# Decoder trunk on one core: scales of the first sub-layer by TensorE products, input load and norm first

## Chip, cores, metric

One core of a Trainium2 chip. The metric is the device time of one execution in microseconds (us), as the median of several runs; for a single execution the profile gives the span from its first to its last instruction.

## The reference

Four layers of a decoder trunk over 256 tokens of width 1024, everything in float32. Each layer has three sub-layers (feed-forward, token mixer, feed-forward). Each sub-layer normalises its input, modulates it with a scale and a shift, computes, normalises again and adds with a gate. Scale, shift and gate are products of silu(c) with slices of a large weight `ada_w` (4 x 1024 x 9216).

```python
cond = jax.nn.silu(c)                                   # (1, 1024)
for i in range(4):
    mod = (cond @ ada_w[i] + ada_b[i]).reshape(B, 3, 3, D)
    def sublayer(x, sidx, fn, res_w):
        shift, scl, gate = mod[:, sidx, 0], mod[:, sidx, 1], mod[:, sidx, 2]   # each [:, None, :]
        hh = rms_norm(x, norm_g[i, 2 * sidx]) * (1.0 + scl) + shift
        return x + res_w * gate * rms_norm(fn(hh), norm_g[i, 2 * sidx + 1])
    x = sublayer(x, 0, lambda hh: swiglu(hh, ffn_w1[i, 0], ffn_w2[i, 0]), 0.5)
    ...
```

What matters here is the very first sub-layer (i = 0, sidx = 0): its shift and scale have to be there before its first matrix product, and nothing runs ahead of it that could hide their making.

## The kernel before, in words

The tokens lie in two halves `h` of 128 (tiles `x0`, `x1`). Every weight is loaded as float32 by the SP queue (`raw_load`, L126, into a ring of 7 buffers of 128x1024, 512 KB each), split by ScalarE into a rounded part `hi` (L135) and by VectorE into the rest `lo` (L136), and multiplied three times on TensorE (hi by yh, hi by yl, lo by yh: L369, L370, L371), where `yh` and `yl` are the same split of the modulated input. A tile framework writes each engine's instructions into one fixed order and sets the semaphores; each engine then runs its own order strictly, and `tc.issue_after` only holds an instruction back in that order.

The start of the program is `Ffn.first` (L465 and on). The conditioning vector is loaded, transposed by TensorE (L85) and put through silu into `cT`, 8 columns of 128 (L86). Five small tiles with norm gains and biases (`g_ld`) come over the ScalarE queue (L104) and are turned by `turn_gains` (five transposes `pt_g` L111, five copies L112 into `abT` and `gT`).

The modulation of the first sub-layer comes in four column blocks `cb` of 512 (0 and 1 the shift, 2 and 3 the scale; 0 and 2 belong to the first half of the width, called n = 0, and 1 and 3 to the second, n = 1). For one block `first_sums(cb)` loads four tiles `raw_ada` of 2 x 128 rows, and VectorE forms the running sum of row times silu(c) in `ada_acc`: eight instructions of 128x512 (the first L265, the others L267). `first_columns` then adds over the partitions on TensorE: four float32 products `p_ada` of a 128x128 piece with a column of ones (L242), and VectorE makes the columns `ab` of them (shift L244; scale L247 and L248).

The input is loaded (L473), `norm_in` squares it on ScalarE (L315), VectorE and GpSimd make the factor `rx` (L307, L308), VectorE the normalised `xn` (L338). TensorE turns it (`p_y`, L322), `modulate` applies `ab` (ScalarE for h = 0, L333; VectorE for h = 1, L331) and splits into `yh` (L334) and `yl` (L335).

With half of the width modulated, half of the products can be done: `products(b, 0)` runs 48 matmuls `p_gu` for each of the first three blocks `b` of the hidden layer (144 in all) over n = 0; in the meantime blocks cb = 1 and 3 are made, n = 1 is modulated, and `products(b, 1)` adds the second half and ends in `hu` (silu on ScalarE, L531).

Of the kernel before, what the change touches and what calls it, by code (L numbers as in the profile page):

```python
# [28 lines left out]
D = 1024  # L29
# [11 lines left out]
def trunk_kernel(ctx, tc, x, c, ada_w, ada_b, norm_g, ffn_w1, ffn_w2, nsa_w_in, nsa_cmp_pe, nsa_cmp_w1,  # L41
# [4 lines left out]
    def dap(t, off, ap):  # L46
        return bass.AP(tensor=t.tensor, offset=t.offset + off, ap=ap)
# [13 lines left out]
    def bank(tag, shape, name):  # L61
        n = {"acc": 4, "mm": 2, "tp": 2}[tag]
        return psum.tile(shape, FT, name=name, tag=tag, bufs=n)
# [58 lines left out]
    def raw_load(ap, shape, name):  # L122
        t = stream.tile([128] + shape, FT, name="raw_" + name, tag="raw", bufs=NRAW)
        aps = ap if isinstance(ap, list) else [(slice(0, 128), ap)]
        for sl, a in aps:
            nc.sync.dma_start(out=t[sl], in_=a)  # L126
        return t
# [106 lines left out]
    def first_columns(cbs):  # L234

        if not AB:
            AB[0, 0] = work.tile([128, 2 * KC], FT, name="ab", tag="ab", bufs=3)
        ab = AB[0, 0]
        for cb, a in cbs:
            p = bank("acc" if cb % 2 == 0 else "tp", [128, 4], "p_ada0")  # L240
            for j in range(4):
                nc.tensor.matmul(p[:, j:j + 1], a[:, j * 128:(j + 1) * 128], ones_col, start=True, stop=True)  # L242
            if cb < 2:
                nc.vector.tensor_add(ab[:, 8 + cb * 4:12 + cb * 4], p, abT[:, cb * 4:cb * 4 + 4])  # L244
            else:
                o = ab[:, cb * 4 - 8:cb * 4 - 4]
                nc.vector.scalar_tensor_tensor(o, p, 1.0, abT[:, cb * 4:cb * 4 + 4], op0=OP.add, op1=OP.add)  # L247
                ins = nc.vector.tensor_mul(o, o, gT[:, cb * 4 - 8:cb * 4 - 4])  # L248
        return ins.ins

    summed = []

    def first_sums(cb):

        a = work.tile([128, 512], FT, name="ada_acc", tag="ada_acc", bufs=NACC)
        for k0 in range(0, KC, 2):
            r = raw_load(dap(ada_w, k0 * 128 * 9 * D + cb * 512, [[9 * D, 128], [128 * 9 * D, 2], [1, 512]]),
                         [2, 512], "ada")
            for j in range(2):
                k = k0 + j  # L260
                with ExitStack() as st:
                    for ins in summed[-1:]:
                        st.enter_context(tc.issue_after(ins))
                    if k == 0:
                        ins = nc.vector.tensor_scalar(a, r[:, j], cT[:, k:k + 1], None, op0=OP.mult)  # L265
                    else:
                        ins = nc.vector.scalar_tensor_tensor(a, r[:, j], cT[:, k:k + 1], a, op0=OP.mult, op1=OP.add)  # L267
                summed.append(ins.ins)
        return a

    def gate_finish(i, s, accs):

# [122 lines left out]
    class Ffn:  # L395
# [70 lines left out]
        def first(self):  # L466

            self.new_hb()
            cbs, xn, ps = {}, [], []
            turn_gains()  # L470
            cbs[0] = first_sums(0)
            for h in range(2):
                nc.sync.dma_start(out=xs[h], in_=x[0, h * 128:(h + 1) * 128, :])  # L473
            cbs[2] = first_sums(2)
            for h in range(2):
                r, _ = norm_in(h)
                xn.append(big([128, D], "xn"))
                for m in range(2):
                    scaled(xn[h], h, m, r)

            def products(b, n):
                for cc in range(2):
                    if not n:
                        ps.append(bank("mm" if b == 0 else "acc", [128, 2, T], "p_gu"))
                    self.gu(ps[2 * b + cc], b, cc, range(KC // 2 * n, KC // 2 * (n + 1)))
                    if n:
                        self.hu(ps[2 * b + cc], b, cc)

            for n in range(2):
                done = summed[-1]  # L490
                gate = first_columns([(cb, cbs[cb]) for cb in (n, n + 2)])
                pt = [turn(xn[h], n) for h in range(2)]
                for h in range(2):
                    modulate(AB[0, 0], pt[h], h, n, h == 1)
                gate_on[:] = [gate] if n else [done]
                if n:
                    products(FIRST - 1, 0)
                    for b in range(FIRST):
                        self.up(b)
                        products(b, 1)  # L500
                else:
                    for b in range(FIRST - 1):
                        self.up(b, part=0)
                        products(b, 0)
                        gate_on[:] = []
                        if not b:
                            cbs[1] = first_sums(1)
                    cbs[3] = first_sums(3)
                    gate_on[:] = [gate]
                    self.up(FIRST - 1, part=0)  # L510
            self.begun = FIRST
            return gate
# [648 lines left out]
```

## Time and profile before

| | us |
|---|---|
| median of 3 runs (2192.07 to 2196.46) | 2192.75 |
| the profiled execution | 2192.57 |
| its span, first to last instruction | 2190.8 |
| TensorE busy in the span (97%) | 2120.4 |
| VectorE, ScalarE busy | 1634.4, 1106.2 |

The span is 1.8 us shorter than the execution around it. Times in the profile are counted from the start of the span. PE is TensorE, PEld its weight loads, DVE is VectorE, ACT is ScalarE, POOL is GpSimd, SP is the engine whose queue issues the weight loads. "idle before" is the time in which an engine stood still ahead of a row, with what released it.

### The profile page before, as it was taken

Reading aid. Unit: us, or ns where it says so; the run is one execution under the profiler, and the core shown is the slowest. Engines: PE = TensorE matmul, PEld = TensorE weight load, DVE = VectorE, ACT = ScalarE, POOL = GpSimd, SP = SyncE. Lnnn points to the kernel's source line nnn. Section 1 sums busy time; section 2 is a strip of 40 time slices with the busy share of each in tenths; the row PEclk is TensorE's granted clock in tenths of the full one; section 3 lists DMA queues with packets and bytes.
Section 4 is the critical chain, followed back from the end, with each engine's and each line's share of the span. In section 5 each row is a group of like instructions: output and inputs, shape, how many; then the busy total and the mean of one; then the engine's idle time right before and its main releaser. Section 6 shows DMA issues by size and latency. Waiting matters only on the chain.

```text
span 2190.8 us, 37402 instructions
## 1 busy us (share of the span) xinstructions
PE 2120.4 (97%) x14427; PEld 1865.7 (85%) x14427; DVE 1634.4 (75%) x2748; ACT 1106.2 (50%) x1965; POOL 69.0 (3%) x154
## 2 busy tenths in 40 slices
PE   5999999999999999999999999999999999999998
PEld 5999866799899979899989888799999997667998
DVE  7987876877798777777687858687778858767654
ACT  3444644644554456744454455664454445555443
POOL 1000000000000000100000000000000000000000
PEclk9999998999999999999999999999999999999999
DMA  9998762588699856388779947278869977625761
GB/s 313 338 347 275 230 170 62 183 287 270 209 328 306 281 192 216 124 284 279 239 253 325 314 161 280 74 256 282 283 188 334 320 230 228 163 71 162 244 199 60
DMA packets 338179, 512.55 MB, mean 234 GB/s; under 512 B 20832, under 2 KB 211256, under 8 KB 338000
## 3 DMA queue, kind: packets, MB, share of 16 engines
q1 hardware_dynamic: 329456, 501.15, 69.2%
q10 hardware_dynamic: 8544, 9.01, 1.4%
q8 instruction: 113, 1.85, 0.3%
q14 instruction: 66, 0.54, 0.1%
HBM read 507.91 MB, written 1.05 MB: 232 GB/s over the span
## 4 chain that ended last, share of the span: by engine, by line
PE 73%; DVE 10%; DMA 6%; issue 5%; ACT 3%; POOL 2%; SPq 0%; ACTq 0%; DVEq 0%; POOLq 0%
PE p_gu L369 11%; PE p_gu L370 11%; PE p_gu L371 11%; PE f L388 6%; PE f L389 6%; PE f L392 6%; DMA raw_ada<-in_ada_w_dram 4%; DVE lo_w L136 3%; PE p_o L818 2%; PE p_s L646 2%; PE p_pr L371 1%; PE p_pr L369 1%; PE p_pr L370 1%; PE p_t L668 1%; DVE ada_acc L192 1%
## 5 line engine op out<-in xcount | busy, mean ns | idle before, releaser
L135 ACT CAST hi_w<-raw_w 128x1024 fp32r<-128x1024 f32 x528 | 551.8, 1054 | 329.1 <-PE f L392 116.2
L136 DVE TENSOR_TENSOR lo_w<-raw_w,hi_w 128x1024 fp32r<-128x1024 f32 x528 | 633.0, 1220 | 103.9 <-ACT hi_w L135 98.4
L369 PE MATMUL p_gu<-yh,hi_w 128*128 128x256 f32 x2368 | 665.8, 281 | 4.0 <-DVE yh L334 4.0
L370 PE MATMUL p_gu<-yl,hi_w 128*128 128x256 f32 x2368 | 661.2, 279 | 0.3 <-DVE yl L335 0.3
L371 PE MATMUL p_gu<-yh,lo_w 128*128 128x256 f32 x2368 | 660.9, 279 | 0.0
L369 PEld LDWEIGHTS p_gu<-yh,hi_w 128*128 128x128 f32 x2368 | 445.9, 188 | 17.3 <-DVE lo_w L136 6.0
L192 DVE SCALAR_TENSOR_TENSOR ada_acc<-raw_ada,cT,ada_acc 128x512 f32<-128x512 f32 x500 | 373.8, 748 | 105.4 <-DMA raw_ada<-in_ada_w_dram 97.3
L370 PEld LDWEIGHTS p_gu<-yl,hi_w 128*128 128x128 f32 x2368 | 446.2, 188 | 5.4 <-issue 1.7
L371 PEld LDWEIGHTS p_gu<-yh,lo_w 128*128 128x128 f32 x2368 | 446.1, 188 | 0.0
L388 PE MATMUL f<-hi_w,hb 128*128 128x512 f32 x704 | 275.7, 393 | 2.5 <-ACT hb L533 2.4
L389 PE MATMUL f<-lo_w,hb 128*128 128x512 f32 x704 | 275.8, 392 | 0.0
L392 PE MATMUL f<-hi_w,hb 128*128 128x512 f32 x704 | 228.2, 391 | 0.0
L533 ACT CAST hb<-sg 128x256 fp32r<-128x256 f32 x148 | 60.2, 407 | 207.8 <-DVE sg L532 206.2
L388 PEld LDWEIGHTS f<-hi_w,hb 128*128 128x128 f32 x704 | 132.2, 188 | 30.1 <-ACT hb L533 5.5
L392 PEld LDWEIGHTS f<-hi_w,hb 128*128 128x128 f32 x704 | 131.6, 188 | 29.1 <-DVE hb L534 1.8
L531 ACT ACTIVATE sg<-p_gu 128x256 f32<-128x256 f32 x148 | 56.2, 380 | 197.5 <-PE p_gu L371 183.2
L389 PEld LDWEIGHTS f<-lo_w,hb 128*128 128x128 f32 x704 | 132.2, 188 | 24.4 <-issue 0.2
L532 DVE TENSOR_TENSOR sg<-sg,p_gu 128x256 f32<-128x256 f32 x148 | 61.5, 415 | 79.5 <-ACT sg L531 79.3
L657 ACT ACTIVATE sc<-sc,sm_m 128x128 f32<-128x128 f32 (+1 forms) x160 | 70.6, 443 | 41.4 <-DVE sm_m L652 41.4
L534 DVE TENSOR_TENSOR hb<-sg,hb 128x256 fp32r<-128x256 f32 x148 | 62.4, 422 | 35.2 <-ACT hb L533 35.2
L333 ACT ACTIVATE y<-p_y,ab 128x128 f32<-128x128 f32 x184 | 67.4, 465 | 33.3 <-PE p_y L322 28.6
L370 PE MATMUL p_pr<-yl,hi_qk 128*128 128x256 f32 x256 | 71.8, 281 | 0.0
(266 smaller groups left out, 3226.6 us busy)
## 6 DMA issues: line engine op xcount, KB each, us to landing
raw_w<-in_ffn_w_dram SPq DMA_DIRECT2D x528, 512.0 KB
raw_ada<-in_ada_w_dram SPq DMA_DIRECT2D x288, 512.0 KB
raw_kv<-in_nsa_w_in_dram SPq DMA_DIRECT2D x16, 512.0 KB
raw_q<-in_nsa_w_in_dram SPq DMA_DIRECT2D x16, 512.0 KB
raw_cw<-in_nsa_cmp_w_dram SPq DMA_DIRECT2D x16, 512.0 KB
raw_wo<-in_nsa_w_out_dram SPq DMA_DIRECT2D x32, 256.0 KB
raw_qk<-in_sb_w_in_dram SPq DMA_DIRECT2D x16, 512.0 KB
raw_qk<-in_diff_w_in_dram SPq DMA_DIRECT2D x16, 512.0 KB
```

What stands on the lines that cost most here:

```text
L135: nc.scalar.copy(hi, src)
L136: nc.vector.tensor_sub(lo, src, hi)
L192: nc.vector.scalar_tensor_tensor(a, r[:, j], cT[:, k:k + 1], a, op0=OP.mult, op1=OP.add)
L333: nc.scalar.activation(y[:, j, :], p[:, j, :], AF.Identity, scale=ab[:, k:k + 1], bias=ab[:, 8 + k:9 + k])
L369: nc.tensor.matmul(o, cols(wh), yh[:, k, :], start=first and k == 0, stop=False)
L370: nc.tensor.matmul(o, cols(wh), yl[:, k, :], start=False, stop=False)
L371: nc.tensor.matmul(o, cols(wl), yh[:, k, :], start=False, stop=last and k == KC - 1)
L388: nc.tensor.matmul(acc[n], lh, wh[:, sl], start=first, stop=False)
L389: nc.tensor.matmul(acc[n], lh, wl[:, sl], start=False, stop=False)
L392: nc.tensor.matmul(acc[n], ll, wh[:, sl], start=False, stop=last)
L534: nc.vector.tensor_sub(hl[:, cc, :], sg, hh[:, cc, :])
L657: nc.scalar.activation(sc[e][:, j, :], sc[e][:, j, :], AF.Exp, bias=m[:, x:x + 1], scale=sl[x], accum_out=l[:, x:x + 1])
```

## The change

Input load and norm move ahead of the modulation weights. The blocks 0 and 2 are loaded in turns (`first_pair`): a tile of block 0, a tile of block 2, and so on. Block 0 is summed on VectorE as before. Block 2 is no longer summed there: for each of its 8 row groups TensorE multiplies the four 128x128 pieces of the raw tile with the column of silu(c), 32 float32 products that add up in one bank `p_mod`, from which `first_columns` takes the scale without a product with ones. The turning of the gains is held back until after the third of the four tiles of block 2. Blocks 1 and 3 are made as before.

```diff
+            if cb == 2:
+                p = a
+            else:
+                p = bank("acc" if cb % 2 == 0 else "tp", [128, 4], "p_ada0")
...
+    def first_pair(then):
+
+        a = work.tile([128, 512], FT, name="ada_acc", tag="ada_acc", bufs=NACC)
+        p = bank("acc", [128, 4], "p_mod")
+        for k0 in range(0, KC, 2):
+            if k0 == KC - 2:
+                with tc.issue_after(ins.ins):
+                    then()
+            first_sum(a, first_load(0, k0), k0)
+            r = first_load(2, k0)
             for j in range(2):
                 k = k0 + j
+                for q in range(4):
+                    ins = nc.tensor.matmul(p[:, q:q + 1], r[:, j, q * 128:(q + 1) * 128], cT[:, k:k + 1],
+                                           start=k == 0 and q == 0, stop=k == KC - 1 and q == 3, skip_group_check=True)
+        return a, p
...
             cbs, xn, ps = {}, [], []
-            turn_gains()
-            cbs[0] = first_sums(0)
             for h in range(2):
                 nc.sync.dma_start(out=xs[h], in_=x[0, h * 128:(h + 1) * 128, :])
-            cbs[2] = first_sums(2)
+            cbs[0], cbs[2] = first_pair(turn_gains)
             for h in range(2):
-                r, _ = norm_in(h)
+                with tc.issue_after(silu):
+                    r, _ = norm_in(h)
```

(`first_load` and `first_sum` are the two halves of the loop of `first_sums`, cut out so that both functions call them.) The change also moves later instructions, since the framework orders each engine anew. Line numbers of the changed kernel are larger: the products are L292, `p_ada` is L245, `ab` L247, L250 and L251, `p_y` L347, `p_gu` L394 to L396.

TensorE's order from the first instruction on, before (`pt_c` turns c):

```order
L85 MATMUL pt_c<-ident,c_67 128x8
L111 MATMUL pt_g<-ident,g_ld 128x96 x5
L322 MATMUL p_y<-ident,xn 128x128 x3
L242 MATMUL p_ada_172<-ones_col,ada_acc 128x1 x4
L322 MATMUL p_y<-ident,xn 128x128 x5
L242 MATMUL p_ada_178<-ones_col,ada_acc 128x1 x4
L369 MATMUL p_gu<-yh,hi_w_211 128x256 x2
```

and in the changed kernel:

```order
L85 MATMUL pt_c<-ident,c_67 128x8
L292 MATMUL p_mod<-cT,raw_ada 128x1 x16
L347 MATMUL p_y<-ident,xn 128x128 x4
L292 MATMUL p_mod<-cT,raw_ada 128x1 x8
L111 MATMUL pt_g<-ident,g_ld 128x96 x5
L347 MATMUL p_y<-ident,xn 128x128 x4
L245 MATMUL p_ada_196<-ones_col,ada_acc 128x1 x4
L292 MATMUL p_mod<-cT,raw_ada 128x1 x8
L394 MATMUL p_gu<-yh,hi_w_230 128x256 x2
```

Thirty-two products stand ahead of the first `p_gu` where four stood (the sums of block 2); the turned gains and all turned inputs stand between them.

VectorE's order before, from the first scale columns to the sums of block 1 (`lo` of the first two weight tiles, then the modulation of n = 0):

```order
L136 TENSOR_TENSOR lo_w_212<-raw_w_209,hi_w_211 128x1024
L247 SCALAR_TENSOR_TENSOR ab<-p_ada_178,abT 128x4
L136 TENSOR_TENSOR lo_w_218<-raw_w_215,hi_w_217 128x1024
L248 TENSOR_TENSOR ab<-ab,gT 128x4
L265 TENSOR_SCALAR ada_acc<-raw_ada,cT 128x512
L331 TENSOR_SCALAR y<-p_y,ab 128x128 x4
L334 CAST yh<-y 128x4x128 x2
L335 TENSOR_TENSOR yl<-y,yh 128x4x128 x2
L267 SCALAR_TENSOR_TENSOR ada_acc<-raw_ada,cT,ada_acc 128x512 x3
```

and in the changed kernel:

```order
L250 SCALAR_TENSOR_TENSOR ab<-p_mod,abT 128x4
L251 TENSOR_TENSOR ab<-ab,gT 128x4
L356 TENSOR_SCALAR y<-p_y,ab 128x128 x4
L359 CAST yh<-y 128x4x128 x2
L360 TENSOR_TENSOR yl<-y,yh 128x4x128 x2
L136 TENSOR_TENSOR lo_w_231<-raw_w_228,hi_w_230 128x1024
L136 TENSOR_TENSOR lo_w_237<-raw_w_234,hi_w_236 128x1024
L267 TENSOR_SCALAR ada_acc<-raw_ada,cT 128x512
L269 SCALAR_TENSOR_TENSOR ada_acc<-raw_ada,cT,ada_acc 128x512 x7
```

The two `lo` of the first weights and the first sum of block 1, which stood ahead of the modulation, now stand behind it. Further down, where n = 1 is modulated, one more `lo` has moved ahead of the last `yl`; VectorE's order there in the changed kernel (`cvalid` is a constant of a later layer):

```order
L251 TENSOR_TENSOR ab<-ab,gT 128x4
L1115 TENSOR_SCALAR cvalid_711<-cdist_709 128x15
L1115 TENSOR_SCALAR cvalid_718<-cdist_716 128x15
L136 TENSOR_TENSOR lo_w_389<-raw_w_386,hi_w_388 128x1024
L356 TENSOR_SCALAR y<-p_y,ab 128x128 x2
L136 TENSOR_TENSOR lo_w_395<-raw_w_392,hi_w_394 128x1024
L359 CAST yh<-y 128x4x128
L356 TENSOR_SCALAR y<-p_y,ab 128x128
L360 TENSOR_TENSOR yl<-y,yh 128x4x128
L356 TENSOR_SCALAR y<-p_y,ab 128x128
L136 TENSOR_TENSOR lo_w_488<-raw_w_485,hi_w_487 128x1024
L359 CAST yh<-y 128x4x128
```

Behind these rows stand `lo_w_494` and the last `yl`; before, the modulation of n = 1 stood in one piece behind `lo_w_469`, the fifth `lo` after the first `yl`, and without the two `cvalid`.

## Rows read from the trace of the kernel before

**Rows 1.** The page: the span, and the engines' busy time, share and instructions.

```profile
span 2190.8 us, 37402 instructions
PE 2120.4 (97%) x14427; PEld 1865.7 (85%) x14427; DVE 1634.4 (75%) x2748; ACT 1106.2 (50%) x1965; POOL 69.0 (3%) x154
```

**Rows 2.** Busy time by stretch; last columns: granted TensorE clock, DMA share, GB/s.

```profile
core 0: us, PE busy (x) PEld busy (x) DVE busy (x) ACT busy (x) POOL busy (x), PEclk, DMA share, GB/s
5.00:10.00 5.00, 0.00 (x0) 0.00 (x0) 4.25 (x6) 0.00 (x0) 1.15 (x17) 1.00 1.06 391
10.00:15.00 5.00, 0.37 (x2) 0.37 (x3) 1.77 (x4) 2.17 (x6) 0.98 (x1) 1.00 1.04 356
30.00:35.00 5.00, 4.75 (x24) 4.75 (x24) 4.93 (x7) 1.05 (x1) 0.00 (x0) 1.00 0.60 156
```

**Rows 3.** TensorE's timeline: start, duration, instruction, count, idle before and releaser.

```profile
14.63 1.17 PE L111 MATMUL pt_g<-ident,g_ld 96*128 96x96 f32 x5 [11.92 <-DMA g_ld<-in_ada_b_dram]
15.59 0.85 PE L322 MATMUL p_y<-ident,xn 128*128 128x128 f32 x3
16.23 1.76 PE L242 MATMUL p_ada<-ones_col,ada_acc 128*128 128x1 f32 x8
17.85 0.45 PE L322 MATMUL p_y<-ident,xn 128*128 128x128 f32 x1
23.34 1.84 PE L242 MATMUL p_ada<-ones_col,ada_acc 128*128 128x1 f32 x8 [3.05 <-DVE ada_acc L267]
29.13 0.77 PE L369 MATMUL p_gu<-yh,hi_w 128*128 128x256 f32 x2 [3.96 <-DVE yh L334]
30.25 0.58 PE L370 MATMUL p_gu<-yl,hi_w 128*128 128x256 f32 x1 [0.35 <-DVE yl L335]
43.28 0.95 PE L242 MATMUL p_ada<-ones_col,ada_acc 128*128 128x1 f32 x8
```

**Rows 4.** The chain that ended last, 0 to 35 us: start, time until the next piece.

```profile
3.25 8.00 DMA x<-in_x_dram
...
31.04 0.21 PE p_gu L369
...
34.81 0.12 PE p_gu L369
```

**Rows 5.** VectorE's timeline, 5 to 51 us.

```profile
5.27 0.49 DVE L265 TENSOR_SCALAR ada_acc<-raw_ada,cT 128x512 f32<-128x512 f32 x1 [4.07 <-DMA raw_ada<-in_ada_w_dram]
5.79 3.94 DVE L267 SCALAR_TENSOR_TENSOR ada_acc<-raw_ada,cT,ada_acc 128x512 f32<-128x512 f32 x5
12.79 0.21 DVE L307 TENSOR_SCALAR rx<-ssx 128x1 f32<-128x1 f32 x1 [3.06 <-ACT junk L315]
25.22 0.16 DVE L247 SCALAR_TENSOR_TENSOR ab<-p_ada,abT 128x4 f32<-128x4 f32 x1 [0.89 <-PE p_ada L242]
25.30 1.22 DVE L136 TENSOR_TENSOR lo_w<-raw_w,hi_w 128x1024 fp32r<-128x1024 f32 x1
26.44 0.15 DVE L248 TENSOR_TENSOR ab<-ab,gT 128x4 f32<-128x4 f32 x1
26.91 1.36 DVE L331 TENSOR_SCALAR y<-p_y,ab 128x128 f32<-128x128 f32 x4
30.11 2.32 DVE L267 SCALAR_TENSOR_TENSOR ada_acc<-raw_ada,cT,ada_acc 128x512 f32<-128x512 f32 x3
50.45 1.29 DVE L335 TENSOR_TENSOR yl<-y,yh 128x512 fp32r<-128x512 f32 x2
58.61 0.25 DVE L1091 TENSOR_SCALAR cvalid<-cdist 128x15 f32<-128x15 f32 x2
```

**Rows 6.** ScalarE's timeline: the first square of x, and the first silu.

```profile
11.28 0.63 ACT L315 ACTIVATE junk<-x 128x512 bf16<-128x512 f32 x1 [8.35 <-DMA x<-in_x_dram]
...
54.92 0.38 ACT L531 ACTIVATE sg<-p_gu 128x256 f32<-128x256 f32 x1 [1.57 <-PE p_gu L371]
```

**Rows 7.** Busy time by stretch, 354 to 358 us, columns as in rows 2.

```profile
354.00:356.00 2.00, 2.00 (x3) 0.39 (x4) 1.91 (x11) 0.00 (x0) 0.00 (x0) 0.50 0.00 0
356.00:358.00 2.00, 2.00 (x4) 0.59 (x4) 0.81 (x5) 0.00 (x0) 0.00 (x0) 0.50 0.00 0
```

More of the change, by code (lines that the diff above doesn't have):

```diff
@@ L239, in first_columns @@
         for cb, a in cbs:
-            p = bank("acc" if cb % 2 == 0 else "tp", [128, 4], "p_ada0")
-            for j in range(4):
-                nc.tensor.matmul(p[:, j:j + 1], a[:, j * 128:(j + 1) * 128], ones_col, start=True, stop=True)
+            if cb == 2:
+                p = a
+            else:
+                p = bank("acc" if cb % 2 == 0 else "tp", [128, 4], "p_ada0")
+                for j in range(4):
+                    nc.tensor.matmul(p[:, j:j + 1], a[:, j * 128:(j + 1) * 128], ones_col, start=True, stop=True)
             if cb < 2:
@@ L251, in trunk_kernel, with first_load, first_sum @@
     summed = []
+    def first_load(cb, k0):
+        return raw_load(dap(ada_w, k0 * 128 * 9 * D + cb * 512, [[9 * D, 128], [128 * 9 * D, 2], [1, 512]]), [2, 512], "ada")
+    def first_sum(a, r, k0):
+        for j in range(2):
+            k = k0 + j
+            with ExitStack() as st:
+                for ins in summed[-1:]:
+                    st.enter_context(tc.issue_after(ins))
+                if k == 0:
+                    ins = nc.vector.tensor_scalar(a, r[:, j], cT[:, k:k + 1], None, op0=OP.mult)
+                else:
+                    ins = nc.vector.scalar_tensor_tensor(a, r[:, j], cT[:, k:k + 1], a, op0=OP.mult, op1=OP.add)
+            summed.append(ins.ins)
     def first_sums(cb):
@@ L256, in first_sums @@
         for k0 in range(0, KC, 2):
-            r = raw_load(dap(ada_w, k0 * 128 * 9 * D + cb * 512, [[9 * D, 128], [128 * 9 * D, 2], [1, 512]]),
-                         [2, 512], "ada")
+            first_sum(a, first_load(cb, k0), k0)
+        return a
+    def first_pair(then):
[7 more added lines that the diff above has]
+            r = first_load(2, k0)
             for j in range(2):
                 k = k0 + j
[L261 to L269, printed above, removed]
+                for q in range(4):
+                    ins = nc.tensor.matmul(p[:, q:q + 1], r[:, j, q * 128:(q + 1) * 128], cT[:, k:k + 1],
+                                           start=k == 0 and q == 0, stop=k == KC - 1 and q == 3, skip_group_check=True)
+        return a, p
     def gate_finish(i, s, accs):
```

## The prediction

> **What bounds the kernel now.** I read the page first, for the whole: TensorE is busy in 2120.4 of 2190.8 us [rows 1]. So only about 70 us of the span are free of it, and a change pays or costs by what it does to the start and the stops of TensorE's stream. Next TensorE's timeline, for the place of the change: the first product `p_gu` starts at 29.13 and the unbroken stream at 30.25 [rows 3]; what stands ahead is the start-up that the change rebuilds. Then the chain from 0 to 35 us, for what sets that start: the wait for x until 11.25 [rows 4], then VectorE's norm and sums, the last four products `p_ada`, the scale, the modulation. VectorE's timeline gives the prices; it is busy for 4.93 of the 5 us from 30 to 35 [rows 2], so behind the start VectorE and TensorE run side by side, and the reader is to keep both in view.
>
> The second half of the width shows how tight that is. The last `yl` starts at 50.45 and ends, with 1.29, at 51.74 [rows 5]. Its products: the first block's silu comes at 54.92 on the end of the first 24 of them [rows 6]; at 0.12 each [rows 4] they began about 51.9. So TensorE needs `yl` just when VectorE has it: **what delays VectorE's second `yl` delays TensorE from there on**, with no cushion.
>
> **The parts of the change.** The profiled execution took 2192.57, 0.18 under the median; the sum is made on 2192.57.
>
> *Loads.* Two x tiles go ahead of the modulation tiles, in SP's queue and on the DMA engines. The first tile has landed at 5.27 [rows 5]; at 356 to 391 GB/s [rows 2] a tile of 0.524 MB takes 1.34 to 1.47 us. The first tile for TensorE is now the fourth in line: 5.2 + 3 x 1.4 = 9.4. All ten tiles land when they did, since the same bytes are ahead of the last.
>
> *Norm.* It gains nothing: the squares stand behind the `g_ld` loads in ScalarE's queue, which wait for earlier loads to land, and `rx` stands in VectorE's order behind four sums of block 0, of which two need the fifth tile (9.4 + 1.4 = 10.8, plus 2 x 0.75): 12.3, against 12.79 [rows 5]. The turned inputs have never been late, so this is worth nothing.
>
> *Products.* 32 are added. The like of one is a row of `p_ada`: same shape, two instructions each. Eight instructions start at 16.23 and the next at 17.85 [rows 3]: 0.405 a product; by the durations, 1.84 for four, 0.46. I take 0.405, from a stream without a stop as this one, and keep 0.46 as the upper end; the lower is the 0.95 for four at 43.28 [rows 3], 0.24, at which TensorE's clock stands at its other level (below, rival one). In between stand, in order, eight turned inputs (three take 0.64 from 15.59 on [rows 3], so 1.7), the five turned gains (0.96 from 14.63 on) and the four `p_ada` of block 0. From 9.4: 36 x 0.405 + 1.7 + 1.0 = 17.3, so 26.7, with the last one's tail **26.8**; the last `p_ada` ended at 25.18 before [rows 3]. Each tile lands before its turn, so nothing interrupts this; and nothing hides it, since the scale waits for the last product. By the Trainium skill (TensorE: Matmul & The Clock Gate, LDWEIGHTS) a load of weights costs by its columns, 107 ns for 128 of them, whatever streams behind: an estimate of 0.21 a product and, for 32, 6.8 in place of 13.0. The trace has 0.405 at this place and 0.24 later; by the page's figure the sum would be that of rival one.
>
> *Sums removed.* VectorE loses the eight sums of block 2, about 0.75 each [rows 5]: 5.7 us. But it then waits for the products: its last sum of block 0 needs tile nine, at 9.4 + 5 x 1.4 = 16.4, and stands behind `rx` and `xn` of the second half and two more sums; I put its end at 19.7, and anything up to 24 would do. The scale comes at 26.8. Seven us idle take the place of 5.7 us of work.
>
> *First modulation.* Before, the scale stood behind one `lo` (25.30 to 26.44 [rows 5]); that wait goes. From `ab` at 26.44 to the end of `yl` at 30.11 took 3.67, with a sum of 0.4 in it [rows 5]: 3.3 now. 26.8 + 0.3 for the first `ab` and its hand-over + 3.3 + 0.2, my allowance for the other hand-overs, = 30.6, against 30.11: **+0.5**. TensorE can do only four `p_gu` by then, since the first `lo` comes behind `yl`, at 31.8.
>
> *VectorE from the first to the second `yl`.* Before: 15 sums, five `lo`, the columns. Now: 16 sums, eight `lo` and the two `cvalid`. A `lo` is 1.14 (25.30 to 26.44), the extra sum the first of its block at 0.49, `cvalid` 0.25 [rows 5]: 3 x 1.14 + 0.49 + 0.25 = **+4.15**. The sums now run as two whole chains, and a sum behind a sum takes 3.94 / 5 = 0.79, not 0.75 [rows 5]; TensorE's order puts `p_ada` of block 1 behind the first 48 `p_gu` and that of block 3 behind the next 48, where VectorE waits for it both times, as it did at one place before: together **+0.75**, my estimate, between 0 and 2.
>
> *Sum.* 0.5 + 4.15 + 0.75 = 5.4. The second `yl` ends near 57.1, the products behind it wait, and from there TensorE's stream is as before. 2192.57 + 5.4 = **2198.0**. With 0.46 a product 36 x 0.055 = 2.0 more: 2200.0. With the tile half a us earlier and the waits at 0: 2196.7. The clock's rise inside the first `p_gu` changes little: they run at 0.21 each, later at 0.12 [rows 4], but wait for VectorE anyway.
>
> *Without cost.* Some of SP's next loads now wait for TensorE to free a tile. The third weight tile waits longest, for the last product at 26.8, but VectorE wants it only behind two `lo` and eight sums, past 38: eleven us, where x took 8.00 from issue to landing [rows 4]. The copies of the gains, now near 22, are needed at 24.
>
> **Rivals.**
>
> *One: TensorE's clock rises during the products; not slower.* `p_gu` runs at 0.21 at 31.04 and at 0.12 at 34.81 [rows 4], that is at 1.2 and 2.4 GHz, 5.7 us after the first of them at 29.13. If the products with silu(c) do the same, TensorE is fast from 15.1: 14 products at 0.405, then 0.24. The rest waits for tiles and for the last sum at 19.7; `p_ada` and eight products are over at 19.7 + 12 x 0.24 = 22.6, 4.2 earlier than 26.8. Then 5.4 - 4.2 = +1.2: 2193.8, within 0.2%. For it: nothing but that the engine is busy without a stop. Against it: from 14.63 to 18.3 it was, with transposes and such products, and the next stream still began at 0.21; and from 354 to 358 the granted clock is 0.50, the lower level, with TensorE busy 4.00 of 4 us [rows 7], so being busy is not enough, and one column behind 128 columns of weights is as little as can stream. By the Trainium skill (TensorE: Matmul & The Clock Gate, Part 1) sustained activity releases the throttle, which would bring this case; rows 7 do not agree with it if busy time is the activity meant.
>
> *Two: the delay is swallowed later.* The other 40 us of TensorE's free time lie at later changes of stage. If one of them waits for loads that keep their own pace, half of it is back: 2195.3. Against it: the loads are issued as buffers come free, by the same delayed VectorE.
>
> *Three: VectorE's 5.7 us pay.* That needs the 32 products to be over when the sums are, at 19.7, so (19.7 - 9.4 - 2.7) / 32 = 0.24 each from the first on; from that price it decides. With `p_ada` behind, 4 x 0.24 = 1.0, the first `yl` ends at 19.7 + 1.0 + 3.8 = 24.5, 5.6 earlier than before, the second 5.6 - 4.9 = 0.7 earlier: 2191.9. Against it: no row ahead of 34 us is that fast.
>
> **The numbers.** Forecast 0.72, rival one 0.15, two 0.08, three 0.05. A difference of 0.2%, 4.4 us, is about what a measurement of this kernel can tell from none: 2188.4 and 2197.1 are its bounds. Of the forecast's 0.72, whose own range is 2196.0 to 2200.4, three quarters lie above 2197.1: slower 0.54. Rivals one to three and the rest of the forecast lie within, less what is left to the other side: 0.41. Faster by so much is left 0.05, for what I overlook. The range goes from rival one's better side, 2192.6, to 2200.4; it leaves out rival three and the far side of the forecast, under 0.2.
>
> **What would show it.** Right: `p_mod` in pairs of 0.2 us, the last over at 26.8 to 29; VectorE idle some 7 us ahead of `ab`; a stop of TensorE of about 1 us ahead of the first `lo` product; the second `yl` ending near 57; the first silu near 60.3 instead of 54.92; idle time of TensorE ahead of block 3's `p_ada` and of the first products with the second `yl`. Wrong: products at 0.24 or less (rival one), or the first silu before 56. If the silu is late and the end is not, it is rival two.

## The result and the profile after

| | before | changed kernel |
|---|---|---|
| median of 10 runs each, us | 2192.47 | 2207.61 |
| ratio, 95% interval | | 1.0061 [1.0038, 1.0084] |
| the profiled execution, us | 2192.57 | 2209.70 |
| its mean granted TensorE clock | 0.991 | 0.987 |

Slower by 15.1 us in the medians, 0.7%, and the interval of the ratio leaves out 1; the forecast was 5.4, and 2207.6 lies above the range. Of the 17.1 us between the two profiled executions, 6.8 are there at the first silu. Another 7.6 come in one stretch of the program 230 us later, where both kernels run as many instructions on each engine, and the last 3 behind that stretch.

**The start.** TensorE's timeline of the changed kernel (columns as in [rows 3]):

```profile
10.18 6.96 PE L292 MATMUL p_mod<-cT,raw_ada 128*128 128x1 f32 x32 [7.62 <-DMA raw_ada<-in_ada_w_dram]
...
17.89 3.41 PE L292 MATMUL p_mod<-cT,raw_ada 128*128 128x1 f32 x16
...
23.12 1.71 PE L245 MATMUL p_ada<-ones_col,ada_acc 128*128 128x1 f32 x8
24.69 3.55 PE L292 MATMUL p_mod<-cT,raw_ada 128*128 128x1 f32 x16
...
31.24 0.80 PE L394 MATMUL p_gu<-yh,hi_w 128*128 128x256 f32 x2 [3.00 <-ACT hi_w L135]
...
58.67 0.38 PE L395 MATMUL p_gu<-yl,hi_w 128*128 128x256 f32 x1 [0.71 <-DVE yl L360]
```

The first product starts at 10.18 (forecast 9.4). Sixteen instructions are eight products: 3.41 for eight, 0.425 each (forecast 0.405), and there is no stop from 10.18 to 28.24 (24.69 + 3.55), where the last one ends (forecast 26.8; `p_ada` ended at 25.18 in [rows 3]). VectorE, to be read against [rows 5]:

```profile
8.17 0.49 DVE L267 TENSOR_SCALAR ada_acc<-raw_ada,cT 128x512 f32<-128x512 f32 x1 [6.98 <-DMA raw_ada<-in_ada_w_dram]
...
11.48 1.54 DVE L269 SCALAR_TENSOR_TENSOR ada_acc<-raw_ada,cT,ada_acc 128x512 f32<-128x512 f32 x2 [2.03 <-DMA raw_ada<-in_ada_w_dram]
12.94 0.21 DVE L332 TENSOR_SCALAR rx<-ssx 128x1 f32<-128x1 f32 x1
...
24.93 0.16 DVE L247 TENSOR_TENSOR ab<-p_ada,abT 128x4 f32<-128x4 f32 x1 [4.31 <-PE p_ada L245]
28.28 0.16 DVE L250 SCALAR_TENSOR_TENSOR ab<-p_mod,abT 128x4 f32<-128x4 f32 x1 [3.18 <-PE p_mod L292]
...
32.17 2.35 DVE L136 TENSOR_TENSOR lo_w<-raw_w,hi_w 128x1024 fp32r<-128x1024 f32 x2
...
57.93 0.69 DVE L360 TENSOR_TENSOR yl<-y,yh 128x512 fp32r<-128x512 f32 x1
```

Its first sum starts 2.9 us later than at 5.27 [rows 5], since two x tiles are ahead of it; it waits for tiles (2.03 in the row at 11.48) and then 4.31 + 3.18 = 7.5 us for TensorE. `rx` comes when it came (12.94, 12.79 before): the norm first has gained nothing. The first modulation is over at 32.17 (forecast 30.6, before 30.11), the second `yl` at 58.62 (57.1, before 51.74), and TensorE stops for it at 58.67. ScalarE, against [rows 6]:

```profile
10.43 0.63 ACT L340 ACTIVATE junk<-x 128x512 bf16<-128x512 f32 x1 [7.65 <-DMA raw_ada<-in_ada_w_dram]
...
61.69 0.39 ACT L555 ACTIVATE sg<-p_gu 128x256 f32<-128x256 f32 x1 [2.73 <-PE p_gu L396]
```

The first silu is at 61.69, 6.8 after the 54.92 of before. The simplest account of this is VectorE's time up to the second `yl` in one row each, before and changed (busy time by stretch, columns as in [rows 2]):

```profile
0.00:51.74 51.74, 29.13 (x200) 27.82 (x201) 40.02 (x72) 18.61 (x34) 7.85 (x71) 1.00 0.96 322
```

```profile
0.00:58.62 58.62, 42.53 (x258) 40.91 (x258) 36.60 (x67) 19.53 (x35) 8.09 (x73) 1.00 0.86 286
```

VectorE is busy for 40.02 of 51.74 and for 36.60 of 58.62: 3.4 us of work less, 10.3 us of waiting more, together the 6.9. (The granted clock has no record ahead of its first rise, at 34.6 and 38.5 us. The 1.00 that these rows, and those of [rows 2], show for earlier times is that missing record and not a reading; the durations there, 0.425 us a product, are those of the lower level. An execution's mean clock counts this time as full speed too.)

**The rest.** The same markers in both programs, one of VectorE ahead of the end of the first token mixer (`qkv<-ks,peT`) and one of ScalarE behind it (the first `sg<-p_gx`), stand at 288.73 and 409.83 before, at 295.31 and 424.01 in the changed kernel: 6.6 behind, then 14.2. The stretch between them (columns as in [rows 2], the granted clock third from the end), before:

```profile
288.73:409.83 121.10, 114.69 (x633) 74.38 (x632) 87.80 (x270) 66.01 (x177) 3.32 (x4) 0.94 0.44 127
```

and in the changed kernel:

```profile
295.31:424.01 128.70, 122.30 (x633) 79.56 (x632) 87.99 (x270) 66.02 (x177) 3.33 (x4) 0.88 0.42 120
```

The counts of instructions are the same, the busy times of VectorE and ScalarE too. TensorE's granted clock differs, 0.94 and 0.88, and its busy time with it, by 7.6 us, as much as the stretch.

From the second marker to the end of the span the changed kernel takes 3.0 us more (1784.0 for 1781.0), at a granted clock of 0.99 in both. The other profiles have 1780.2 for the kernel before (e1) and 1782.0, 1780.6 and 1782.2 for the changed one (e5, e11, e13). So part of the 3.0 is the single execution; whether the rest belongs to the change, these six do not show.

### The profile page after: what moved, and what is told of

Same layout as the page of the kernel before. It is cut to its first block, busy times and chain, and to the rows that moved or that the text cites. A ratio compares the mean times of both kernels' runs of the same rounds, so it can differ in the third digit from the quotient of the medians.

```text
span 2208.0 us, 37508 instructions
## 1 busy us (share of the span) xinstructions
PE 2142.4 (97%) x14483; PEld 1884.1 (85%) x14483; DVE 1628.9 (74%) x2740; ACT 1105.5 (50%) x1965; POOL 66.5 (3%) x154
## 4 chain that ended last, share of the span: by engine, by line
PE 73%; DVE 10%; DMA 6%; issue 5%; ACT 3%; POOL 2%; SPq 0%; DVEq 0%; POOLq 0%; ACTq 0%
PE p_gu L394 11%; PE p_gu L396 11%; PE p_gu L395 11%; PE f L413 6%; PE f L414 6%; PE f L417 6%; DMA raw_ada<-in_ada_w_dram 5%; DVE lo_w L136 3%; PE p_o L842 2%; PE p_s L670 2%; PE p_pr L396 2%; PE p_pr L394 2%; PE p_pr L395 2%; PE p_t L692 1%; DVE ada_acc L192 1%
## 5 line engine op out<-in xcount | busy, mean ns | idle before, releaser
L394 PE MATMUL p_gu<-yh,hi_w 128*128 128x256 f32 x2368 | 666.0, 282 | 3.0 <-ACT hi_w L135 3.0
L396 PE MATMUL p_gu<-yh,lo_w 128*128 128x256 f32 x2368 | 661.6, 280 | 0.8 <-DVE lo_w L136 0.7
L394 PEld LDWEIGHTS p_gu<-yh,hi_w 128*128 128x128 f32 x2368 | 446.1, 189 | 16.4 <-DVE lo_w L136 6.0
L396 PEld LDWEIGHTS p_gu<-yh,lo_w 128*128 128x128 f32 x2368 | 446.2, 189 | 1.7 <-DVE lo_w L136 1.7
```

Source lines behind the costliest of these rows:

```text
L394: nc.tensor.matmul(o, cols(wh), yh[:, k, :], start=first and k == 0, stop=False)
L396: nc.tensor.matmul(o, cols(wl), yh[:, k, :], start=False, stop=last and k == KC - 1)
```

## Experiments

The theory (T): the start-up costs a fixed 6.8 us, through 32 slow products on the path and what VectorE waits for them; what the medians showed beyond it is TensorE's clock. The open part of it has two sides: the clock of the single execution (C), or something that the changed kernel brings with it (D). T, C, N and the other letters are those of the expectations. Each experiment's runs have runs of the kernel before beside them. The first silu is that of one profile: 54.92 and 55.45 in two of the kernel before, 60.74 to 61.69 in four of the changed one. The runs of e6, e8 and e9 have a mean clock that can't be compared, since their clock rises and falls within the start-up already.

| | silu at, us | median, us | before beside it, us | ratio, 95% |
|---|---|---|---|---|
| e1 before again | 55.45 | 2194.63 | 2194.04 | 1.0000 [0.9985, 1.0014] |
| e2 loads and norm first | 55.44 | 2194.27 | 2194.04 | 1.0002 [0.9984, 1.0020] |
| e3 products alone | 66.85 | 2208.80 | 2194.04 | 1.0065 [1.0042, 1.0088] |
| e4 repeated `p_ada` | 60.51 | 2200.84 | 2194.04 | 1.0026 [1.0009, 1.0042] |
| e5 changed kernel | 61.68 | 2198.52 | 2190.76 | 1.0042 [1.0022, 1.0063] |
| e6 wide products | 63.37 | 2198.72 | 2190.76 | 1.0028 [1.0006, 1.0051] |
| e7 `lo` ahead | 58.59 | 2198.26 | 2190.76 | 1.0025 [1.0003, 1.0046] |
| e8 operands exchanged | 58.03 | 2206.95 | 2190.76 | 1.0059 [1.0038, 1.0080] |
| e9 wide in between | 64.20 | 2204.18 | 2194.81 | 1.0045 [1.0025, 1.0065] |
| e10 half by products | 54.54 | 2188.58 | 2194.81 | 0.9972 [0.9951, 0.9993] |
| e11 changed kernel | 60.90 | 2199.47 | 2194.81 | 1.0029 [1.0006, 1.0051] |
| e12 e10 again | 53.53 | 2193.51 | 2191.83 | 1.0008 [0.9987, 1.0029] |
| e13 changed kernel | 60.74 | 2199.75 | 2191.83 | 1.0044 [1.0028, 1.0060] |

**e1, the kernel before again.** No edit.

> The kernel before, unchanged, once more, for its spread and its granted clock. Theory T (the start-up of the changed kernel costs a fixed 6.8 us; what comes on top of it is time at the lower clock level that the delayed program meets in the first mixer): this kernel stays near 2192 us with a mean granted clock near 0.991, and its profile has the first mixer (300 to 390 us) at the lower level for about 14 us. Rival C (time at the lower level in the first mixer is chance and meets both kernels alike): its runs spread as those of the changed kernel do, between 0.985 and 0.993, and their median lies between 2192 and 2200 us.

Its runs spread from 2187.65 to 2200.65 with clocks of 0.987 to 0.993, their median between 2192 and 2200. As rival C has it, the kernel before meets such executions too. T's clock was nearly met as well (0.9904 for 0.991), so this run alone does not part the two.

**e2, input load and norm first, alone.**

```diff
             cbs, xn, ps = {}, [], []
-            turn_gains()
-            cbs[0] = first_sums(0)
             for h in range(2):
                 nc.sync.dma_start(out=xs[h], in_=x[0, h * 128:(h + 1) * 128, :])
+            turn_gains()
+            cbs[0] = first_sums(0)
             cbs[2] = first_sums(2)
             for h in range(2):
-                r, _ = norm_in(h)
+                with tc.issue_after(silu):
+                    r, _ = norm_in(h)
```

(The last two lines, which hold the norm behind silu(c) in each engine's order, are part of the change too.)

> The part of the change that puts the input load and the norm first, alone; both blocks are summed on VectorE as before. The only difference is the place of the two input loads in SP's queue. Theory T: nothing is gained and nothing lost, the squares start near 10.4 us as in the changed kernel or near 11.3 as before, the last ada tile lands when it did, first silu at 54.9 (+-0.5), total 2192.5 (+-2). Rival N (the norm first is what delays): first silu 2 us or more later than 54.92, total 2195 or more.

First silu 55.44 against 55.45 in e1: this part costs and brings nothing. Rival N is out.

**e3, products alone**, the loads in the order of before.

```diff
-            cbs[2] = first_sums(2)
+            cbs[2] = first_products()
```

(`first_products` is the part of `first_pair` on block 2; `first_columns` takes its bank as in the changed kernel.)

> The products with silu(c) for block 2 alone, with the loads in the order of before (block 0, input, block 2), so TensorE can begin with block 2 only at its first tile, near 13.7 us. Theory T (32 products at 0.425 us each on the path ahead of the scale): 13.7 + 32 x 0.425 = 27.3, and with eight turned inputs and the four products of block 0 in between 30.5 to 31; scale 2.5 us later than in the changed kernel, first silu between 62 and 65 us (7 to 10 over before), total 2200 to 2204 with the clock of before, more by what the first mixer loses to the clock. Rival N (the norm first delays, not the products): first silu below 58, total below 2197.

First silu 66.85, 11.9 behind before, two us more than expected; the median, 2208.80, is nearly 5 above its forecast too. TensorE's timeline of e3:

```profile
16.38 6.98 PE L287 MATMUL p_mod<-cT,raw_ada 128*128 128x1 f32 x32
...
30.15 3.41 PE L287 MATMUL p_mod<-cT,raw_ada 128*128 128x1 f32 x16
```

The products start at 16.38, not 13.7, as they stand behind the turned gains and an input in TensorE's order, and end at 33.56. So the products carry the cost without the new order of the loads; with the loads in turns and the input first the changed kernel has 5 us less of it.

**e4, a delay of TensorE and nothing else.** The kernel before, with the last four `p_ada` done four times; every other row of every engine stays.

```diff
-            for j in range(4):
+            for j in 4 * list(range(4)) if cb == 2 else range(4):
```

> The kernel before with the four products that make the scale from block 2 done four times over (the same result): 12 more one-column float32 products, everything else in the same order on every engine. Theory T: 12 x 0.41 = 4.9 us more on TensorE ahead of the scale, of which 1.2 replace the wait behind lo: ab near 30.3 instead of 26.44, first yl and second yl 3.7 to 3.9 later, first silu near 58.7, and a constant 3.8 from there to 300 us. Rival D (any delay of this size moves the first mixer into more time at the lower clock level, as in the changed kernel): then 5 us or more on top behind 300 us, total 2200 or more, mean clock 0.988 or less. Rival C (that time is chance): total 2196.3 (+-2), clock as in the unchanged kernel of the same call.

VectorE's timeline of e4:

```profile
30.34 0.16 DVE L247 SCALAR_TENSOR_TENSOR ab<-p_ada,abT 128x4 f32<-128x4 f32 x1 [6.01 <-PE p_ada L242]
...
56.04 1.28 DVE L335 TENSOR_TENSOR yl<-y,yh 128x512 fp32r<-128x512 f32 x2
```

The scale comes 5.1 us later than at 25.22 [rows 5], as forecast, and all of it reaches the second `yl` (56.04 for 50.45): the `lo` that I had counted as a cushion starts behind the scale, not ahead of it. First silu +5.6, where 3.8 was expected. The median is 6.8 over, above 2200 as D had it, but at a mean clock of 0.992 against 0.990 for before: a delay of this size does not by itself bring the lower clock. Rival D, in that form, is out.

**e5, e11, e13, the changed kernel again.** No edit.

> The changed kernel, unchanged, once more, beside the kernel before in the same call. Theory C (the time that the first mixer spends at the lower clock level differs from execution to execution, in both kernels; the profiled execution of the changed kernel was one with much of it): mean granted clock as that of the kernel before, within 0.001, median 7 to 9 us over before (2201 to 2204), and the new profile has its first mixer 6.9 +- 1.5 us behind before's, not 14. Rival D (the change itself brings the first mixer more time at the lower level): mean clock again 0.9885 or less, median 12 us or more over before.

> The changed kernel a third time, beside before in the same call. Theory C (the start-up costs 6.8 us always; more than that is the clock of the single execution, which both kernels have alike): first silu 61.7 (+-0.2), mean granted clock within 0.001 of before's in this call, median 7 to 9.5 us over before. Rival D (the delayed program is brought to the lower level more often): mean clock at least 0.002 under before's in this call, median 11 us or more over.

> The changed kernel a fourth time. At the clock of 0.990 its runs so far stand at 2202.7, 2202.5 and 2201.7 us and those of before at 2194.8, 2194.3 and 2195.1, 7 to 8 us apart, while the medians stood 15, 7.8 and 4.7 apart. Theory C (fixed 7 to 8 us and the clock of single executions): first silu 61.7, 7 to 8 us apart again at equal clock, mean clock within 0.001 of before's. Rival D (the lower clock of the first set comes again): mean clock 0.002 or more under before's, median 11 us or more over.

The stretch between the two markers in e5, then in e13:

```profile
295.06:412.57 117.51, 111.25 (x633) 73.69 (x632) 87.68 (x270) 65.95 (x177) 3.32 (x4) 0.97 0.46 131
```

```profile
295.38:425.29 129.91, 123.56 (x633) 80.07 (x632) 88.00 (x270) 65.89 (x177) 3.32 (x4) 0.87 0.43 118
```

One kernel, the same instructions: 117.51 us at a clock of 0.97, 129.91 at 0.87. With the four profiles of the changed kernel, 116.9 to 129.9; with two of before, 121.1 and 120.0. So the stretch that holds 7.6 us of the first difference is one that the changed kernel itself runs 12 us faster in another execution. The mean clocks of e5, e11 and e13, changed kernel and before beside it, are 0.9912 and 0.9910, 0.9906 and 0.9900, 0.9899 and 0.9909. The 46 runs of the changed kernel and 127 of before whose clock is known give

| | runs | median, us | mean clock | at a clock of 0.990, us | us for 0.001 of clock |
|---|---|---|---|---|---|
| before | 127 | 2193.4 | 0.9905 | 2194.6 | 1.9 |
| changed | 46 | 2200.6 | 0.9901 | 2202.1 | 2.0 |

(the last two columns from a straight line through the runs; they scatter about it by 2.3 and 1.8 us, one standard deviation). The change costs about 7.5 us at equal clock, 7.2 between the medians. The medians of e5, e11 and e13 stand 7.8, 4.7 and 7.9 over before: 4.7 is less than C expected, 11 or more, as D has it, came in none, nor did D's 0.002 of clock. The first ten runs, at 15.1 us, had 0.9884; a line through them alone gives 2202.7 at 0.990. Their median lies 4.9 above that, and the median of before beside them 2.1 under the 2194.6 of the table, at clocks that are not on record: with the 8.1 at equal clock that is the 15.1.

This comparison is not good to a microsecond for every kernel. e4, whose silu came 5.6 later, stands about 9 over the runs of before beside it at equal clock, and e7 below, whose silu came 3.7 later, about 6.5. So time arises behind the start that the clock does not account for; no run says where.

The first silu of e11 and e13 came 0.8 and 1.0 us sooner than expected: the clock's first rise, at 37.4 and 36.4 for 38.5, shifts from one execution of the kernel to the next.

**e6, wide products ahead and between.**

```diff
+    def warm(n, after):
+        for _ in range(n):
+            with tc.issue_after(after):
+                after = nc.tensor.matmul(p_warm, wide[:, 0:128], wide, start=True, stop=True).ins
+        return after
+    warmed = warm(36, pt_c)
...
+            if k0 < KC - 2:
+                w = warm(6, ins.ins)
```

> The changed kernel with 36 wide products (128x256, a result that nobody reads) on TensorE between the turned conditioning vector and the first product with silu(c), and 6 more behind each of the first three tiles' eight products; the order of everything else is the same on every engine. Theory T (the 32 products are slow since TensorE stands at its lower level, and what has to stream to leave it is columns, not instructions): the clock rises ahead of 10 us, the products take 0.24 in place of 0.425, the last is over at 23.9 (20.6 for the last sum of block 0, 0.3, four products p_ada 1.0, eight products 1.9) in place of 28.24, first silu near 57 in place of 61.69, total 4 us or more under the changed kernel. Rival K (the price is the load of weights at any clock, or the clock does not rise): the products stay at 0.4 or more, the wide ones push them back, the last is over past 30, first silu past 63.

TensorE's timeline of e6, and its busy time by stretch (the granted clock is third from the end):

```profile
9.64 1.92 PE L306 MATMUL p_mod<-cT,raw_ada 128*128 128x1 f32 x16 [1.17 <-DMA raw_ada<-in_ada_w_dram]
...
13.11 3.57 PE L306 MATMUL p_mod<-cT,raw_ada 128*128 128x1 f32 x16 [0.73 <-DMA raw_ada<-in_ada_w_dram]
...
26.73 3.55 PE L306 MATMUL p_mod<-cT,raw_ada 128*128 128x1 f32 x16
```

```profile
9.60:12.40 2.80, 2.73 (x22) 2.56 (x22) 0.84 (x2) 2.42 (x7) 0.00 (x0) 1.00 1.06 370
12.40:31.00 18.60, 17.17 (x81) 17.09 (x81) 6.90 (x15) 1.59 (x8) 2.04 (x4) 0.50 0.78 270
```

Half of each theory. The clock did rise ahead of 10 us (at 5.6, during the wide products), and the first eight products took 0.24 each (1.92 / 8). At 12.4 it fell, while TensorE was 2.73 of 2.80 us busy with products and wide ones, and the other 24 took 0.43 to 0.45; the last is over at 30.3. So the price goes with the clock, 0.24 in place of 0.425 where it is up; but a TensorE busy with these products did not keep it up. The first silu, 63.37, came as K had it.

**e7, the two `lo` ahead of the scale.**

```diff
+            if cb == 2:
+                for ins in los[-2:]:
+                    st.enter_context(tc.issue_after(ins))
...
+                if not n:
+                    gate_on[:] = [done]
+                    self.up(0, part=0)
                 gate = first_columns([(cb, cbs[cb]) for cb in (n, n + 2)])
```

> The changed kernel with the two lo of the first weight tiles held ahead of the scale in VectorE's order, where it waits for the products. Theory T (VectorE's work between the two yl has grown by lo's that were pushed behind the modulation, while VectorE stands idle for 7.5 us ahead of it): the two lo fill 2.3 us of that idle time, the second yl ends 2.3 us earlier (56.3 in place of 58.62), first silu 59.4 in place of 61.69 (+-0.8), total 2 to 3 us under the changed kernel. Rival P (the delay is the products alone and VectorE's order does not matter): first silu within 0.5 of 61.69.

VectorE's timeline of e7:

```profile
24.52 2.36 DVE L138 TENSOR_TENSOR lo_w<-raw_w,hi_w 128x1024 fp32r<-128x1024 f32 x2
27.75 0.16 DVE L256 SCALAR_TENSOR_TENSOR ab<-p_mod,abT 128x4 f32<-128x4 f32 x1 [0.88 <-PE p_mod L299]
```

The wait ahead of the scale falls from 3.18 to 0.88, the first silu comes 3.1 us sooner than in the first profile of the changed kernel, a little more than expected, and 2.2 to 3.1 sooner than in all four. Rival P is out: VectorE's order was a third to a half of the start-up's cost (6.8). The two `lo` are not the whole of it: the products of e7 start 0.5 us sooner, at 9.65, and in its order sums of block 1 and the second modulation stand elsewhere too. The median hardly moves (2198.26, e5 2198.52); at equal clock it is 1.4 lower, less than the start gained. This part stayed unclear.

**e8, the operands exchanged**: the row streams, silu(c) is the weight.

```diff
-                for q in range(4):
-                    ins = nc.tensor.matmul(p[:, q:q + 1], r[:, j, q * 128:(q + 1) * 128], cT[:, k:k + 1],
...
+                ins = nc.tensor.matmul(p, cT[:, k:k + 1].to_broadcast([128, 32]), r[:, j], start=k == 0, stop=k == KC - 1)
```

> The changed kernel with the operands of the products exchanged: silu(c) (one column, given 32 times) is the weight and a row group of 512 columns of the raw tile streams, 8 products in place of 32; the row that comes out is copied by ScalarE and turned by four small transposes. Theory T (streaming columns lets the clock rise, one column behind 128 columns of weights does not): the clock rises within some 7 us of the first of them, at 17 us or before, and the two products of the last tile, behind the sums of block 0, take under 1 us each: scale near 25, first silu between 56.5 and 58.5. Rival K (the clock does not rise with this either): it rises first in the p_gu, past 30, the products stay at 1.7 us each, first silu between 59 and 61.

TensorE's timeline of e8:

```profile
15.85 1.91 PE L291 MATMUL p_mod<-raw_ada,cT 128*32 128x512 f32 x4 [0.30 <-DMA raw_ada<-in_ada_w_dram]
...
20.66 1.77 PE L245 MATMUL p_ada<-ones_col,ada_acc 128*128 128x1 f32 x8 [1.90 <-DVE ada_acc L269]
22.36 3.62 PE L291 MATMUL p_mod<-raw_ada,cT 128*32 128x512 f32 x4
```

The clock rose at 13.9, during the streaming rows, as T had it, and fell at 20.7, after a pause of 1.9 us ahead of the `p_ada`, with TensorE busy for 4.44 of the 6.80 us in between; so two row products took 1.91 at one level and 3.62 at the other, and T's "under 1 us each" for the last two did not come. The silu, 58.03, is within its forecast. The median, 2206.95, is not explained by the start: 9 of the 12 runs had a mean clock of 0.981 to 0.987 (the start-up's 17 us at the lower level, from 20.7 to 37.8, make 0.004 of that), and the profiled one ran the stretch between the markers in 129.8 us at 0.87, as e13 did.

**e9, a wide product behind every product**, on e7.

```diff
+                    w = warm(1, ins.ins)
```

> The kernel of e7 (the two lo ahead of the scale) with 44 wide products ahead of the first product with silu(c) and one wide product (128x256, a result that nobody reads) behind each of the 32. In e6 the clock rose at 5.6 and fell again at 12.4, after 8 products at 0.24 each and with six wide ones per tile. Theory T (a one-column product counts for nothing, only streamed columns keep the clock up): with a wide one behind every product the higher level lasts through the products, a pair of them takes 0.35 (0.24 and 0.11) and the last is over near 25 in place of 27.7; first silu between 55 and 56.5 in place of 58.59 in e7. Rival K (the mixture is still too little): the clock falls between 12 and 20 as in e6, a pair takes 0.64, the last product is over past 30, first silu past 60.

TensorE's timeline of e9, one pair at either level:

```profile
10.30 0.28 PE L313 MATMUL p_mod<-cT,raw_ada 128*128 128x1 f32 x2
10.44 0.36 PE L101 MATMUL p_warm<-wide 128*128 128x256 f32 x1
10.64 0.28 PE L313 MATMUL p_mod<-cT,raw_ada 128*128 128x1 f32 x2
...
13.49 0.42 PE L313 MATMUL p_mod<-cT,raw_ada 128*128 128x1 f32 x2
13.78 0.56 PE L101 MATMUL p_warm<-wide 128*128 128x256 f32 x1
14.13 0.42 PE L313 MATMUL p_mod<-cT,raw_ada 128*128 128x1 f32 x2
```

A pair took 0.34 up to 12.6, where the clock fell, and 0.64 after it. Rival K: from 9.88 on TensorE ran without a stop, with a wide product in every pair, and the clock fell nevertheless. Theory T is refuted; what makes the clock fall here, no run shows.

**e10 and e12, half of block 2 by products**: two of its tiles, early, under VectorE's sums; the other two are summed as before and added to the same bank by four products with ones.

```diff
+            first_sum(a0, first_load(0, k0), k0)
+            if k0 < KC // 2:
+                r = first_load(2, k0)
...
+        for k0 in range(KC // 2, KC, 2):
+            first_sum(a2, first_load(2, k0), k0, KC // 2)
...
+            if cb == 2:
+                st.enter_context(tc.issue_after(los[0]))
```

> Half of block 2 by products: TensorE makes 16 products with silu(c) from its first two tiles, early, while VectorE still sums block 0; VectorE sums the other two tiles, and four products with ones add that sum to the same bank. The input loads come behind the third tile of block 0, and one lo is held ahead of the scale. Theory T (the start ends when VectorE has done its work and its waiting up to the second yl: 40.0 busy and 11.7 idle of 51.74 before, 36.6 and 22.0 of 58.62 in the changed kernel; products that are over before the sums cost nothing): VectorE loses 4 sums, 3 us, and waits no longer than before, since 16 x 0.425 = 6.8 end near 14; last sum near 21, scale near 23, second yl between 48.7 and 51.5, first silu between 52 and 54.7, total 0.5 to 3 us under the kernel before. Rival Q (any product with silu(c) delays, or what VectorE gains in work it loses again in waits for tiles): first silu at 55 or later, total the same as before or above.

> The kernel of e10 once more (half of block 2 by products that lie under VectorE's sums). In e10 its first silu came at 54.54, 0.4 before that of the kernel before, its median was 6.2 us under, and its mean granted clock 0.0024 over before's. Theory T (the start-up decides, the clock of single executions is chance): first silu 54.5 (+-0.3) again, mean clock within 0.001 of before's, median 0 to 2 us under before. Rival G (this order of the start brings the first mixer less time at the lower level): mean clock 0.002 or more over before's again, median 4 us or more under.

TensorE's timeline of e10, then its row for VectorE's time up to the second `yl`:

```profile
6.74 6.96 PE L296 MATMUL p_mod<-cT,raw_ada 128*128 128x1 f32 x32 [4.19 <-DMA raw_ada<-in_ada_w_dram]
...
21.81 1.86 PE L248 MATMUL p_mod<-ones_col,ada_acc 128*128 128x1 f32 x8 [1.30 <-DVE ada_acc L275]
```

```profile
0.00:50.16 50.16, 35.33 (x219) 33.71 (x220) 36.14 (x69) 17.30 (x33) 7.75 (x73) 1.00 0.97 326
```

Sixteen products at the same 0.43 each are over at 13.7, under the sums of block 0; the scale waits 0.8 us, for the last four products with ones and not for them. The second `yl` ends at 50.16, 1.6 before that of the kernel before: 36.14 busy and 14.0 idle, for 40.02 and 11.7; of 3.9 us of work taken away, 2.3 went into waits for tiles. The silus are 0.4 and 1.4 us sooner than 54.92 (the clock's first rise was at 34.8 and 32.7). The median was 6.2 under before in e10 (clock 0.9924 against 0.9900) and 1.7 over in e12 (0.9895 against 0.9909). At a clock of 0.990 the 24 runs stand at 2193.8, before at 2194.6. In e12 none of the forecasts came: not G's clock, and T's silu (54.5), clock (within 0.001) and median (0 to 2 under) were missed by 1.0 us, 0.0014 and 1.7 us over. So this version is as fast as before and no faster that a measurement could tell; the gain of e10 is not claimed.

## Why the prediction was wrong

Against its own steps:

- **Loads.** The first tile for TensorE at 9.4: 10.18. Mis-sized by 0.8; the third tile, at 8.17, kept to 1.4 us a tile, the fourth came 2.0 after it.
- **Norm.** Worth nothing: right (`rx` at 12.94, forecast 12.3, before 12.79; e2).
- **Products.** 0.405 each: 0.425, 0.7 us over all 36. With the 0.8, the last over at 28.2 for 26.8. This is the failing term of the start, 1.4 us. That they would stay at the slow level was right, rival one fell. By the Trainium skill (TensorE: Matmul & The Clock Gate, LDWEIGHTS) a load of 128 columns takes 107 ns; with two loads a product that is an estimate of 0.21. It was not met here: 0.425, and 0.24 where the clock was up (e6).
- **Sums removed.** Seven us idle in place of 5.7 us of work: 7.5. About right.
- **First modulation.** +0.5: +2.1 (32.17 for 30.11), the 1.4 of the products and 0.2.
- **First to second `yl`.** +4.15 and +0.75 of waits, 4.9: +4.8 (58.62 less 32.17 is 26.4, before 21.6). Right, and in its parts: VectorE's busy time grew by 4.4 (19.97 of 21.63 before, 24.36 of 26.45), its waits by 0.4.
- **Sum.** +5.4 at the first silu: +6.8 (5.8 and 6.0 in e13 and e11).
- **"From there TensorE's stream is as before."** This step failed. Up to 295 us it held: the distance to the kernel before is 6.6 there. But the stream's pace behind it is not a constant of the program. The first mixer took 128.7 us at a mean clock of 0.88 in the profiled execution, 7.6 more than before, and 116.9 in e11. The rows that showed it were in the prediction [rows 7]: a granted clock of 0.50 with TensorE wholly busy. I read them only as an argument against rival one, not as a term that comes out differently in every execution. My range held the uncertain costs of the start and nothing for this, though the three runs of before already lay 4.4 us apart. At equal clock the 7.5 would make 2200.1, just inside a range whose ends (2192.6 and 2200.4) lie beyond the values that I worked out (2193.8 and 2200.0) without a reason given.

Rival two (the delay swallowed later) was not borne out, rival three neither. What all runs together give, 7.2 to 7.5 us, is nearer to the forecast than the first 15, and lies above it by 2, of which the products are 1.4. Beside the first silu of the four profiles (5.8 to 6.8 late) 0.7 to 1.7 us are left; what they are, no run settles. Nor do the runs settle why the clock of e8 was low in most of its executions, whether the four sets of the changed kernel differ by more than chance in their clock, or why e4's clock stood above before's.

## What to carry to other kernels

Where one engine's work and waits up to a fixed point set the end of a start-up, count both: work taken off it is worth what it does not turn into waiting, and products handed to TensorE showed no cost of their own where they ended under the sums (e10), while the first silu came 11.9 us later where they ended behind them (e3). Before a difference in the medians is explained, compare a stretch with the same instructions in both profiles, its length beside its granted clock; here 15.1 us between two medians became 7.5 at equal clock. A range should hold the spread that single executions of the same kernel show.

## What the runs showed of the hardware that was not expected

- A product with one column, 128 x 128 float32, costs 0.425 us at the lower clock level (1.2 GHz) and 0.24 at the upper (2.4 GHz); a float32 product with 512 columns, 32 columns of weights, 1.81 and 0.95 (e8).
- TensorE's clock fell while the engine was busy for 2.73 of 2.80 us with products and wide products (e6), and with a wide product in every pair (e9). With wide products alone, from 2.5 us on, it had risen at 5.6 (e6) and 5.8 us (e9).
- The same 121 us of program took 116.4 to 129.9 us in twelve profiled executions of seven kernels, at mean clocks of 0.99 to 0.87, with TensorE busy for 94 to 95% of it.
- Over the runs of one kernel 0.001 of mean clock goes with 1.9 to 2.0 us; the runs scatter about that line by 2.3 us (127 runs of the kernel before) and 1.8 us (46 of the changed one).
